# Decays as one exponential with masks as products, and reciprocal roots by GpSimd's power, in the second layer

## The chip, the cores and the metric

The kernel runs on one core of one Trainium2 chip. The metric is the device time of one execution in microseconds, as the median of several runs. The core has five engines that run their own instruction streams in order and wait for each other by semaphores: TensorE (PE, its weight loads shown as PEld), VectorE (DVE), ScalarE (ACT), GpSimd (POOL) and SyncE (SP, here only an issuer of DMAs).

## The reference

One inference step of two layers over 1088 frames: 1024 of a new stream and 64 of a running one, width 1024. The first layer (gated convolution and band attention) is not touched. The second is a gated delta rule with 8 heads of 128 in chunks of 64 frames:

```
q, k = l2norm(q) * 128**-0.5, l2norm(k)          # x * rsqrt(sum(x*x) + 1e-6)
gc = cumsum(g)                                    # g <= 0, within a chunk
decay[i, j] = exp(gc[i] - gc[j]) for j <= i, else 0
a = strictly lower part of beta[i] * (k k^T) * decay
u, w from solving (a + I) x = [v * beta, k * beta * exp(gc)]
u = u - w S
o = (q * exp(gc)) S + ((q k^T) * decay) u
S = exp(gc_last) * S + (k * exp(gc_last - gc))^T u
o = rmsnorm(o, onorm) ; y = (o * silu(z)) @ w_out  # rmsnorm: x * rsqrt(mean(x*x) + 1e-6) * onorm
```

What is computed must be seen: y of both streams, the caches of the first layer, the last convolution inputs and the state S of the second.

## The kernel before

Activations lie with features on the partitions and frames along the free axis, in three groups of 384, 384 and 320 frames. Every projection splits weights and inputs in a rounded and a remainder part and runs three matmuls per block of 128 x 128 (rows `pjt<-hhi,whi`, `pjt<-hlo,whi`, `pjt<-hhi,wlo`); these make up most of TensorE's work.

The mixer of the second layer takes its 8 heads as four pairs (p = 0 to 3, one head on each half of the partitions) and the 17 chunks of a pair in three batches of 6, 6 and 5 (`BATCHES`). Its steps are generators, and a class `Order` writes TensorE's instruction order out by hand: every step says after which others it may run, has a rank (a lower one goes first), and says with `yield ns` how long it leaves TensorE to others; the estimated time goes on with each matmul. The projections (`main`, rank 5) fill what the steps leave. TensorE keeps exactly this order; the orders of the other engines are made by the scheduler from its own estimate of times. All engines run their orders strictly, so an instruction that waits holds all behind it.

The steps, with the lines that the change and the prediction touch:

- `gates` (from line 885): cumulative decays gc and their exponentials for all pairs.
- `decays` (rank 3, after gates): for each pair and batch, VectorE multiplies gc with an identity (L926), a matmul with a block of ones spreads it over the rows into a bank "tr" of PSUM, VectorE subtracts gc into SBUF (`df`, L930), and for each of the two masks GpSimd adds or subtracts a mask of 0 and -1e30 (L933), ScalarE takes Exp (L934) and issues the write to DRAM (`Dd`, L935). The first is the decay for rows of a (j < i, called Dst), the second its transpose for q k^T (j >= i, called DT). The scratch tiles have one buffer each.
- `prepare` (rank 2, after the decays of its pair): loads Dst and DT through SP's queue, transposes k and q of the batch into "tr" banks, ScalarE sums their squares (`ss`, L976) and copies k (kt), VectorE scales k (kd). Then VectorE takes the reciprocal root of ss by a bit trick and three Newton steps (`rsqrt`, L774 to L780), forms the factors sT, sA and kap (L985 to L987), GpSimd scales kt (L988), TensorE forms k k^T and k q^T in a "tr" bank, and VectorE reads it into An (L997) and KQD (L998) with the decays. Af gathers the diagonal blocks of 16 (L1002, L1004) and goes to DRAM.
- `substitute`: reads the blocks back (AL) and inverts them on GpSimd in 28 small instructions (L1022, L1023), and writes them out again.
- `join`: reads them (Xf, X) and joins blocks of 16 to 64 with small matmuls.
- `solve`: forms u and w of all chunks.
- `scan` (rank 1): the recurrence over the chunks; each chunk's output o gets its sum of squares on ScalarE (`so`, L1144).
- `finish` (rank 3): for up to four chunks, forms the factor of rmsnorm together with q's norm: three VectorE instructions (L1200 to L1202), the bit trick on VectorE, three Newton steps on GpSimd (L782 to L785, twelve instructions), one more on VectorE (L1204); VectorE scales o (L1206), TensorE transposes it, ScalarE multiplies onorm in, and the result goes to DRAM.

The banks "tr" have two buffers, and all steps take them in turn: TensorE can write the next but one only when the engines have read out the present one.

Of the kernel before, what the change touches and what calls it, by code (L numbers as in the profile page):

```python
# [7 lines left out]
F32 = mybir.dt.float32  # L8
F32R = mybir.dt.float32r
I32 = mybir.dt.int32  # L10
AF = mybir.ActivationFunctionType
# [28 lines left out]
C_M1, C_M2 = 448, 512  # L40
# [16 lines left out]
def constants():  # L57
# [10 lines left out]
    c[:, C_M1:C_M1 + 64] = np.where(j[None, :] < i[:, None], 0.0, NEG)  # L68
    c[:, C_M2:C_M2 + 64] = np.where(j[None, :] >= i[:, None], 0.0, NEG)
# [38 lines left out]
class Net:  # L108
# [124 lines left out]
    def run(self):  # L233
# [4 lines left out]
        with tc.tile_pool(name="pj", bufs=2, space=PSUM) as self.pj:  # L238
# [15 lines left out]
            self.Dd = [dram.tile([P, NCH, 64], F32, name=f"Dd{i}") for i in range(8)]  # L254
# [505 lines left out]
    def odd(self):  # L760
# [12 lines left out]
        def rsqrt(out, x, tmp, eng):  # L773
            dve.tensor_scalar(out.bitcast(I32), x.bitcast(I32), 1, None, ALU.logical_shift_right)  # L774
            dve.tensor_scalar(out.bitcast(I32), out.bitcast(I32), -1, 0x5F3759DF, ALU.mult, ALU.add)  # L775
            for _ in range(3):
                if eng is dve:
                    dve.scalar_tensor_tensor(tmp, out, -0.5, x, ALU.mult, ALU.mult)
                    dve.tensor_tensor(tmp, tmp, out, ALU.mult)
                    dve.scalar_tensor_tensor(out, tmp, 1.5, out, ALU.add, ALU.mult)  # L780
                else:
                    pool.tensor_tensor(tmp, out, out, ALU.mult)  # L782
                    pool.tensor_tensor(tmp, tmp, x, ALU.mult)
                    pool.tensor_scalar(tmp, tmp, -0.5, 1.5, ALU.mult, ALU.add)
                    pool.tensor_tensor(out, out, tmp, ALU.mult)  # L785

# [125 lines left out]

        def decays():
            gc = G["gc"]
            buf = G["buf"]

            def part(i, m):
                return buf[:, 384 * i:384 * i + 64 * m].rearrange("p (c j) -> p c j", j=64)

            for p in range(4):  # L920
                yield 0
                for c0, m in BATCHES:
                    sh = [P, m, 64]
                    gcb = gc[:, p, c0:c0 + m].unsqueeze(2).broadcast_to(sh)
                    gx, df = part(0, m), part(1, m)
                    dve.tensor_tensor(gx, gcb, cst[:, C_ID64:C_ID64 + 64].unsqueeze(1).broadcast_to(sh), ALU.mult)  # L926
                    yield 900
                    ps = pst("tr")
                    self.mm(ps[:, :64 * m], cst[:, C_BD:C_BD + P], gx.rearrange("p c j -> p (c j)"))
                    dve.tensor_tensor(df, ps[:, :64 * m].rearrange("p (c j) -> p c j", j=64), gcb, ALU.subtract)  # L930
                    for q, (cm, op) in enumerate(((C_M1, ALU.subtract), (C_M2, ALU.add))):
                        dx = part(2 + q, m)
                        pool.tensor_tensor(dx, cst[:, cm:cm + 64].unsqueeze(1).broadcast_to(sh), df, op)  # L933
                        act.activation(dx, dx, AF.Exp)  # L934
                        nc.scalar.dma_start(Dd[2 * p + q][:, c0:c0 + m, :], dx)  # L935
                    yield 2500
                order.done.add(f"dec{p}")
# [4 lines left out]
        def zeroed():  # L942
            for name, w in (("Cb", 32), ("BD", P)):
                Z[name] = self.kp.tile([P, NBM, w], F32, name=name)
                pool.memset(Z[name], 0.0)

        def prepare(p, b):
# [3 lines left out]
            yield 4000 if b == 0 else 0  # L951
# [13 lines left out]
            rr = self.kp.tile([P, 2, NBM], F32, name="rr", tag="rr", bufs=3)[:, :, :nb]  # L965
# [398 lines left out]
```

## Time and profile before

| what | value |
|---|---|
| median of 3 runs | 1439.04 us (1437.8 to 1440.11) |
| profiled execution | 1441.69 us, its span 1439.9 us |
| TensorE busy | 1367.9 us, 95% of the span |
| VectorE, ScalarE, GpSimd busy | 867.4, 676.3, 304.9 us |
| mean clock granted to TensorE | 0.982 |
| mixer of the second layer | about 690 to 1310 us |
| decays within it (L926 to L935) | 691 to 774 us |

Times in a row are microseconds from the start of the span, and its length; a bracket at the end of a row tells how long the engine sat idle before it and whose end released it. "x" is the number of instructions. L12 is line 12 of the kernel; L119 and L124 are the helpers through which every matmul and transpose goes, so there the names of the tiles tell them apart.

### The profile page before, as it was taken

The numbers are of one execution on the slowest core, as the hardware profiler recorded it, in microseconds if no ns is written. First come the engines' busy times: TensorE is split into PE (matmuls) and PEld (weight loads), VectorE is DVE, ScalarE is ACT, GpSimd is POOL, SyncE is SP. The second block draws the span as 40 slices with busy tenths as digits, with TensorE's granted clock in tenths as the row PEclk, the third lists the DMA queues.
The fourth block names the chain that finished last, engine by engine and source line by source line (L and its number), as shares of the span: only waits on it lengthen the run. The fifth ranks groups of instructions, "written<-read, shape, count | busy, mean of one in ns | idle before, by whom it ended". The sixth has DMA issues, their size and how long they took to land. (4 is left out here: it accounts for less than half of the span.)

```text
span 1439.9 us, 28413 instructions
## 1 busy us (share of the span) xinstructions
PE 1367.9 (95%) x10600; PEld 1231.2 (86%) x10600; DVE 867.4 (60%) x2496; ACT 676.3 (47%) x1776; POOL 304.9 (21%) x805
## 2 busy tenths in 40 slices
PE   8999999999999999899889999999898989999996
PEld 6989998998999899788768777778786778889995
DVE  7675257237425754777787768666765765433554
ACT  7643345144334455676445554545443534333652
POOL 4001000000100014321235325140524151410222
PEclk9999999999999999999988999999999999999998
DMA  8403111210211274541433112121311142336753
GB/s 267 138 17 90 57 53 45 87 53 27 78 58 47 65 237 140 174 165 38 110 83 67 42 40 70 31 60 33 68 34 42 39 99 61 104 107 219 228 198 117
DMA packets 113834, 132.73 MB, mean 92 GB/s; under 512 B 35280, under 2 KB 80792, under 8 KB 113696
## 3 DMA queue, kind: packets, MB, share of 16 engines
q1 hardware_dynamic: 82448, 104.32, 24.8%
q10 hardware_dynamic: 31248, 26.60, 5.7%
q8 instruction: 83, 1.36, 0.4%
q14 instruction: 55, 0.45, 0.1%
HBM read 99.71 MB, written 34.31 MB: 93 GB/s over the span
## 5 line engine op out<-in xcount | busy, mean ns | idle before, releaser
L119 PE MATMUL pjt<-hhi,wlo 128*128 128x384 f32 (+1 forms) x1768 | 616.9, 349 | 2.8 <-DVE wlo L165 2.8
L119 PE MATMUL pjt<-hhi,whi 128*128 128x384 f32 (+1 forms) x1768 | 583.7, 330 | 10.0 <-ACT whi L164 4.8
L119 PE MATMUL pjt<-hlo,whi 128*128 128x384 f32 (+1 forms) x1768 | 575.9, 329 | 1.0 <-DVE hlo L418 0.9
L119 PEld LDWEIGHTS pjt<-hhi,wlo 128*128 128x128 f32 x1768 | 337.1, 191 | 27.0 <-issue 11.9
L119 PEld LDWEIGHTS pjt<-hhi,whi 128*128 128x128 f32 x1768 | 337.2, 191 | 16.6 <-ACT whi L164 5.8
L119 PEld LDWEIGHTS pjt<-hlo,whi 128*128 128x128 f32 x1768 | 335.5, 190 | 1.9 <-DVE hlo L418 1.9
L165 DVE TENSOR_TENSOR wlo<-wf,whi 128x512 fp32r<-128x512 f32 x222 | 152.5, 710 | 165.4 <-ACT whi L164 164.1
L164 ACT CAST whi<-wf 128x512 fp32r<-128x512 f32 x222 | 130.1, 619 | 166.9 <-PE pjt L119 122.4
L639 ACT ACTIVATE pr<-pr,mx 128x640 f32<-128x640 f32 (+5 forms) x72 | 50.9, 707 | 89.4 <-DVE mx L638 88.8
L811 DVE SCALAR_TENSOR_TENSOR kq<-pjt,par,kq 128x384 f32<-128x384 f32 (+2 forms) x144 | 71.6, 497 | 2.9
L600 POOL MEMSET bias<- 64x64 f32 x8 | 1.5, 182 | 320.7 <-DMA bias<-Gd 295.5
L375 POOL TENSOR_TENSOR sqa<-sqa,sq 128x384 f32<-128x384 f32 (+1 forms) x36 | 39.9, 1109 | 138.0 <-ACT sq L372 137.9
L636 DVE CUSTOM_DVE_ANT_0 pr<-sc,bias 128x640 f32<-128x640 f32 (+5 forms) x72 | 47.9, 666 | 26.8 <-PE sc L119 25.9
L1022 POOL TENSOR_TENSOR px<-AL 48x14 f32<-48x14 f32 (+6 forms) x168 | 46.1, 274 | 61.0 <-DMA AL<-Sd 52.0
L1185 DVE SCALAR_TENSOR_TENSOR S<-S,egl,su 128x128 f32<-128x128 f32 x128 | 40.6, 342 | 30.0 <-PE su L119 29.6
L782 POOL TENSOR_TENSOR so<-so 128x4 f32<-128x4 f32 (+2 forms) x72 | 17.1, 238 | 176.0 <-DVE so L775 117.6
L976 ACT ACTIVATE junk<-tr 128x128 f32<-128x128 f32 x136 | 37.7, 277 | 34.0 <-PE tr L124 28.9
L1023 POOL TENSOR_TENSOR AL<-AL,px 48x14 f32<-48x14 f32 (+6 forms) x168 | 46.2, 275 | 9.4
L124 PE MATMUL pt<-cst,pr 128*128 128x128 f32 (+1 forms) x280 | 43.3, 270 | 4.4 <-DVE pr L641 2.9
L1144 ACT ACTIVATE junk<-o 128x128 f32<-128x128 f32 x68 | 21.0, 309 | 50.8 <-DVE o L1140 40.9
L119 PE MATMUL pjt<-mhi,whi 128*128 128x384 f32 x128 | 43.0, 336 | 1.1 <-ACT whi L164 1.1
L119 PE MATMUL pjt<-mhi,wlo 128*128 128x384 f32 x128 | 43.0, 336 | 0.5 <-DVE wlo L165 0.5
(257 smaller groups left out, 2192.0 us busy)
## 6 DMA issues: line engine op xcount, KB each, us to landing
wf<-in_w_in SPq DMA_DIRECT2D x128, 256.0 KB, 3.7
wf<-in_w_out SPq DMA_DIRECT2D x96, 256.0 KB, 3.2
mf<-mixd SPq DMA_DIRECT2D x31, 192.0 KB, 4.5
x<-in_x SPq DMA_DIRECT2D x8, 384.0 KB, 5.8
xg<-in_x SPq DMA_DIRECT2D x2, 1536.0 KB
xd<-xg SPq DMA_DIRECT2D x2, 1536.0 KB
Dd<-dbuf ACTq DMA_DIRECT2D x16, 192.0 KB, 3.6
od<-o ACTq DMA_DIRECT2D x12, 256.0 KB, 2.3
```

The costliest lines, as they stand in the source:

```text
L119: return self.pe.matmul(out, lhsT=lhsT, rhs=rhs, start=start, stop=stop, **k)
L124: return self.pe.transpose(out, in_, self.ident[0:k, 0:k])
L164: self.act.copy(out=hi, in_=x)
L165: (eng or self.dve).tensor_tensor(lo, x, hi.bitcast(F32), ALU.subtract)
L375: pool.tensor_tensor(acc, acc, sq, ALU.add)
L636: dve.tensor_tensor_reduce(out=cut(pr[0:nq, :nk]), in0=sc[0:nq, :nk // nw, :nw], in1=cut(b["bias"][a][0:nq, j0:j0 + nk]), scale=1.0, scala ...
L639: act.activation(pr[0:nq, :nk], pr[0:nq, :nk], AF.Exp, bias=mx[0:nq, 1:2], scale=1.0, accum_out=mx[0:nq, 2:3])
L811: dve.scalar_tensor_tensor(oi, ch(ps[:, i0 + j + 1:i0 + j + 1 + m]), cw[j], oi, ALU.mult, ALU.add)
L976: act.activation(junk, ps[:, i, :], AF.Square, accum_out=ss[:, a, i0 + i:i0 + i + 1])
L1022: pool.tensor_tensor(t, AL[:, j + 1:16, j:j + 1].broadcast_to([lanes, m, w]), x.broadcast_to([lanes, m, w]), ALU.mult)
L1023: pool.tensor_tensor(o, o, t, ALU.add)
L1185: dve.scalar_tensor_tensor(Sn[:, q, :], S[:, q, :], egl[:, q, p, c:c + 1], su[q], ALU.mult, ALU.add)
```

## The change

The decay becomes one matrix per pair and batch, E = exp(-|gc_j - gc_i|), which serves both triangles, and the masks become products of 0 and 1:

- the subtraction writes back into its PSUM bank, ScalarE takes Abs from there to SBUF, and Exp with scale -1 in place;
- for pairs 1 to 3, `decays` writes E to DRAM once, with three scratch tiles in turn, and `prepare` loads it once; for pair 0, `prepare` computes E itself in its own tile, and waits for `gates` only;
- KQD starts as E times the upper mask, on GpSimd, and is multiplied with k q^T in place; An takes E unmasked, and Af is multiplied with the strictly lower mask of a 16 x 16 block on VectorE (later steps use only the blocks of An below the diagonal).

The reciprocal roots are taken by GpSimd with the operation `pow` and an exponent of -0.5 from a constant tile: one addition and one power in `prepare` for k, and the same in `finish`, where q's norm no longer needs a root of its own: rmsnorm's factor is (mean(o*o) + eq) ** -0.5 with eq = 128 * 1e-6 * (sum(q*q) + 1e-6). The mean's 1/128 moves into the scale of ScalarE's square.

```diff
-    c[:, C_M1:C_M1 + 64] = np.where(j[None, :] < i[:, None], 0.0, NEG)
-    c[:, C_M2:C_M2 + 64] = np.where(j[None, :] >= i[:, None], 0.0, NEG)
+    c[:, C_LOW:C_LOW + 16] = j[None, :16] < (i % 16)[:, None]
+    c[:, C_UP:C_UP + 64] = j[None, :] >= i[:, None]
...
+        def decay(e, gx, p, c0, m):
+
+            sh = [P, m, 64]
+            gcb = G["gc"][:, p, c0:c0 + m].unsqueeze(2).broadcast_to(sh)
+            dve.tensor_tensor(gx, gcb, cst[:, C_ID64:C_ID64 + 64].unsqueeze(1).broadcast_to(sh), ALU.mult)
+            yield 900
+            ps = pst("tr")[:, :64 * m]
+            self.mm(ps, cst[:, C_BD:C_BD + P], gx.rearrange("p c j -> p (c j)"))
+            ps = ps.rearrange("p (c j) -> p c j", j=64)
+            dve.tensor_tensor(ps, ps, gcb, ALU.subtract)
+            act.activation(e, ps, AF.Abs)
+            act.activation(e, e, AF.Exp, scale=-1.0)
+
         def decays():
...
-            for p in range(4):
-                yield 0
+            for p in range(1, 4):
                 for c0, m in BATCHES:
-                    gx, df = part(0, m), part(1, m)
-                    dve.tensor_tensor(gx, gcb, cst[:, C_ID64:C_ID64 + 64].unsqueeze(1).broadcast_to(sh), ALU.mult)
-                    yield 900
-                    ps = pst("tr")
-                    self.mm(ps[:, :64 * m], cst[:, C_BD:C_BD + P], gx.rearrange("p c j -> p (c j)"))
-                    dve.tensor_tensor(df, ps[:, :64 * m].rearrange("p (c j) -> p c j", j=64), gcb, ALU.subtract)
-                    for q, (cm, op) in enumerate(((C_M1, ALU.subtract), (C_M2, ALU.add))):
-                        dx = part(2 + q, m)
-                        pool.tensor_tensor(dx, cst[:, cm:cm + 64].unsqueeze(1).broadcast_to(sh), df, op)
-                        act.activation(dx, dx, AF.Exp)
-                        nc.scalar.dma_start(Dd[2 * p + q][:, c0:c0 + m, :], dx)
+                    e = piece(2 + i % 3, m)
+                    yield from decay(e, piece(i % 2, m), p, c0, m)
+                    nc.scalar.dma_start(Dd[p][:, c0:c0 + m, :], e)
+                    i += 1
                     yield 2500
...
+            Z["root"] = self.kp.tile([P, 1], F32, name="root")
+            pool.memset(Z["root"], -0.5)
...
         def prepare(p, b):
-            yield 4000 if b == 0 else 0
-            Dst, DT = bt("Dst", 64), bt("DT", 64)
-            nc.sync.dma_start(Dst, Dd[2 * p][:, c0:c0 + nb, :])
-            nc.sync.dma_start(DT, Dd[2 * p + 1][:, c0:c0 + nb, :])
+            E, An, KQD = bt("E", 64), bt("An", 64, 2), bt("KQD", 64, 3)
+            if p:
+                nc.sync.dma_start(E, Dd[p][:, c0:c0 + nb, :])
+            else:
+                yield from decay(E, An, p, c0, nb)
+            if b == 0:
+                yield 4000
...
-            dve.tensor_scalar(ss, ss, EPS, None, ALU.add)
-            rsqrt(rr, ss, tmp, dve)
+            dve.tensor_scalar(eq, ss[:, 1, :], EPS, 128.0 * EPS, ALU.add, ALU.mult)
+            pool.tensor_scalar(rk, ss[:, 0, :], EPS, None, ALU.add)
+            pool.tensor_tensor(rk, rk, Z["root"].broadcast_to([P, nb]), ALU.pow)
...
+            pool.tensor_tensor(KQD, E, cst[:, C_UP:C_UP + 64].unsqueeze(1).broadcast_to([P, nb, 64]), ALU.mult)
...
-                dve.tensor_tensor(KQD[:, i0:i0 + m, :], ps[:, :m, 64:128], DT[:, i0:i0 + m, :], ALU.mult)
+                dve.tensor_tensor(KQD[:, i0:i0 + m, :], ps[:, :m, 64:128], KQD[:, i0:i0 + m, :], ALU.mult)
...
+            dve.tensor_tensor(Af, Af, cst[:, C_LOW:C_LOW + 16].unsqueeze(1).broadcast_to([P, nb, 16]), ALU.mult)
...
-                act.activation(junk, o4[:, a, :], AF.Square, accum_out=so[:, 0, a:a + 1])
+                act.activation(junk, o4[:, a, :], AF.Square, scale=128.0 ** -0.5, accum_out=so[:, 0, a:a + 1])
...
         def finish(p, b, i0, m, o4, so):
-            rq = R[p, b]["rq"][:, i0:i0 + m]
-            va, fa, tm = so[:, 0, :m], so[:, 1, :m], so[:, 2, :m]
-            dve.scalar_tensor_tensor(va, va, 1.0 / (128.0 * 128.0), rq, ALU.mult, ALU.mult)
-            dve.tensor_tensor(va, va, rq, ALU.mult)
-            dve.tensor_scalar(va, va, EPS, None, ALU.add)
-            rsqrt(fa, va, tm, pool)
-            dve.scalar_tensor_tensor(fa, fa, 128.0 ** -0.5, rq, ALU.mult, ALU.mult)
+            fa = so[:, 1, :m]
+            pool.tensor_tensor(fa, so[:, 0, :m], R[p, b]["eq"][:, i0:i0 + m], ALU.add)
+            pool.tensor_tensor(fa, fa, Z["root"].broadcast_to([P, m]), ALU.pow)
...
-                order.add(f"prep{n}", 2, prepare(p, b), [f"dec{p}"] + after("prep", n - 1) + after("wy", n - 2) + after("scan", n - 3))
+                order.add(f"prep{n}", 2, prepare(p, b), [f"dec{p}" if p else "gates"] + after("prep", n - 1) + after("wy", n - 2) + after("scan", n - 3))
```

More of the change, by code (lines that the diff above doesn't have):

```diff
@@ L39 @@
 C_ID64 = 384
-C_M1, C_M2 = 448, 512
+C_LOW, C_UP = 448, 512
 C_B16 = 576
@@ L253, in run @@
             self.Gd = [dram.tile([P, LROW], F32, name=f"Gd{h}") for h in range(8)]
-            self.Dd = [dram.tile([P, NCH, 64], F32, name=f"Dd{i}") for i in range(8)]
+            self.Dd = [dram.tile([P, NCH, 64], F32, name=f"Dd{i}") for i in range(4)]
             self.Sd = [[dram.tile([m, P, 16], F32, name=f"Sd{a}{b}") for b, (c0, m) in enumerate(BATCHES)] for a in range(2)]
@@ L771, in comp @@
             return self.kp.tile([P, 4, NCH], F32, name=name)
[L773 to L785, printed above, removed]
         def ch(x):
@@ L981, in prepare @@
                     yield 2160
-            dve.tensor_scalar(ss, ss, EPS, None, ALU.add)
-            rsqrt(rr, ss, tmp, dve)
-            sT, sA, kap = small("sT"), small("sA"), small("kap")
-            dve.tensor_tensor(sT, beta[:, p, c0:c0 + nb], rr[:, 0, :], ALU.mult)
-            dve.scalar_tensor_tensor(sA, sT, -1.0, rr[:, 0, :], ALU.mult, ALU.mult)
-            dve.scalar_tensor_tensor(kap, egc[:, p, c0:c0 + nb], -1.0, rr[:, 0, :], ALU.mult, ALU.mult)
+            sT, sA, kap, rk, eq = (small(x) for x in ("sT", "sA", "kap", "rk", "eq"))
+            dve.tensor_scalar(eq, ss[:, 1, :], EPS, 128.0 * EPS, ALU.add, ALU.mult)
+            pool.tensor_scalar(rk, ss[:, 0, :], EPS, None, ALU.add)
+            pool.tensor_tensor(rk, rk, Z["root"].broadcast_to([P, nb]), ALU.pow)
+            dve.tensor_tensor(sT, beta[:, p, c0:c0 + nb], rk, ALU.mult)
+            dve.scalar_tensor_tensor(sA, sT, -1.0, rk, ALU.mult, ALU.mult)
+            dve.scalar_tensor_tensor(kap, egc[:, p, c0:c0 + nb], -1.0, rk, ALU.mult, ALU.mult)
             pool.tensor_tensor(kt, kt, kap.unsqueeze(2).broadcast_to([P, nb, P]), ALU.mult)
-            An, KQD = bt("An", 64, 2), bt("KQD", 64, 3)
+            pool.tensor_tensor(KQD, E, cst[:, C_UP:C_UP + 64].unsqueeze(1).broadcast_to([P, nb, 64]), ALU.mult)
             for i0 in range(0, nb, 4):
@@ L996, in prepare @@
                 for i in range(m):
-                    dve.scalar_tensor_tensor(An[:, i0 + i, :], ps[:, i, 0:64], sA[:, i0 + i:i0 + i + 1], Dst[:, i0 + i, :], ALU.mult, ALU.mult)
-                dve.tensor_tensor(KQD[:, i0:i0 + m, :], ps[:, :m, 64:128], DT[:, i0:i0 + m, :], ALU.mult)
+                    dve.scalar_tensor_tensor(An[:, i0 + i, :], ps[:, i, 0:64], sA[:, i0 + i:i0 + i + 1], E[:, i0 + i, :], ALU.mult, ALU.mult)
+                dve.tensor_tensor(KQD[:, i0:i0 + m, :], ps[:, :m, 64:128], KQD[:, i0:i0 + m, :], ALU.mult)
                 yield 510
@@ L1004, in prepare @@
                 dve.scalar_tensor_tensor(Af, An[:, :, 16 * j:16 * j + 16], cst[:, C_B16 + j:C_B16 + j + 1], Af, ALU.mult, ALU.add)
+            dve.tensor_tensor(Af, Af, cst[:, C_LOW:C_LOW + 16].unsqueeze(1).broadcast_to([P, nb, 16]), ALU.mult)
             sa = Sd[0][b]
             nc.sync.dma_start(sa.rearrange("c r j -> r c j"), Af)
-            R[p, b] = dict(kd=kd, kt=kt, KQD=KQD, rq=rr[:, 1, :], An=An, sT=sT)
+            R[p, b] = dict(kd=kd, kt=kt, KQD=KQD, eq=eq, An=An, sT=sT)
             yield 0
@@ L1154, in scan @@
                     o4 = self.kp.tile([P, 4, P], F32, name="o4", tag="o4", bufs=3)
-                    so = self.kp.tile([P, 3, 4], F32, name="so", tag="so", bufs=3)
+                    so = self.kp.tile([P, 2, 4], F32, name="so", tag="so", bufs=3)
                 c = c0 + i
```

9 lines of the change are left out of this document (2 added, 7 removed).

## The prediction

> **What bounds the kernel now.** I read the page first, then the windows of the two parts of the second layer's mixer, then who waited for whom on TensorE, then the timelines around its longest gaps.
>
> ```profile
> span 1439.9 us, 28413 instructions
> PE 1367.9 (95%) x10600; PEld 1231.2 (86%) x10600; DVE 867.4 (60%) x2496; ACT 676.3 (47%) x1776; POOL 304.9 (21%) x805
> 690.00:772.00 82.00, 65.90 (x358) 57.98 (x357) 65.64 (x165) 40.73 (x118) 35.50 (x55) 0.88 0.34 94
> 772.00:1310.00 538.00, 516.14 (x5148) 434.02 (x5147) 340.32 (x1243) 235.70 (x790) 166.55 (x642) 0.98 0.25 61
> ```
>
> TensorE bounds: its order is written out, and the steps that the diff touches run between 690 and 1310 us. The change keeps TensorE's number of matmuls (twelve of the decays, as before), so it can only act through TensorE's idle time and its clock. The columns after the length are TensorE, weight loads, VectorE, ScalarE, GpSimd, then the clock. While the decays run (690 to 772) TensorE is idle for 82.0 - 65.9 = 16.1 us and its clock is 0.88; in the rest of the mixer it is idle for 21.9 us of 538. These 38 us and the slow clock are all there is to win.
>
> Who ends the waits, first while the decays run, then behind them (us in total, times, longest):
>
> ```profile
> PE tr L124 <- DVE KQD L998: 3.4, 1, 3.4
> PE tr L124 <- DVE dbuf L930: 3.4, 2, 2.6
> PE tr L119 <- DVE KQD L998: 3.3, 1, 3.3
> PE tr L119 <- ACT junk L976: 2.8, 2, 2.2
> PE tr L119 <- DVE dbuf L926: 1.5, 2, 1.1
> ...
> PE tr L124 <- DVE o L1206: 4.5, 2, 3.0
> PE su L119 <- DVE us L1171: 4.0, 2, 2.7
> PE tr L124 <- DVE KQD L998: 2.4, 3, 1.2
> PE tr L124 <- ACT M L1081: 2.2, 2, 1.4
> PE tr L119 <- DVE KQD L998: 1.3, 5, 0.3
> ```
>
> Most name a "tr" bank of PSUM (two buffers) that a later step of prepare, decays or finish has not yet read out. TensorE's timeline shows what a long one costs beside itself:
>
> ```profile
> 733.20 0.30 PE L119 MATMUL pjt<-hhi,whi 128*128 128x320 f32 x1
> 733.35 0.31 PE L119 MATMUL pjt<-hlo,whi 128*128 128x320 f32 x1
> 737.09 1.09 PE L124 MATMUL tr<-cst,kq 128*128 128x128 f32 x4 [3.44 <-DVE KQD L998]
> 738.25 0.47 PE L119 MATMUL pjt<-hhi,whi 128*128 128x320 f32 x1
> 738.51 0.47 PE L119 MATMUL pjt<-hlo,whi 128*128 128x320 f32 x1
> ...
> 742.46 0.79 PE L124 MATMUL tr<-cst,kq 128*128 128x128 f32 x4
> ...
> 762.15 1.62 PE L119 MATMUL tr<-dbuf,cst 128*128 128x384 f32 x2 [3.29 <-DVE KQD L998]
> 766.45 0.45 PE L119 MATMUL pjt<-hhi,whi 128*128 128x320 f32 x1
> 766.71 0.33 PE L119 MATMUL pjt<-hlo,whi 128*128 128x320 f32 x1
> ```
>
> Matmuls that started 0.15 us apart start 0.26 us apart behind the 3.44 us gap, until about 742.7; behind the 3.29 us gap the same until about 766.6. Each slow stretch loses 44% of its length: 5.6 x 0.44 = 2.5 and 4.45 x 0.44 = 2.0 us.
>
> **Part 1: the roots of prepare.** The path from the sums of squares to the release of the bank, on VectorE, and GpSimd beside it:
>
> ```profile
> 728.51 0.17 DVE L774 TENSOR_SCALAR rr<-ss 128x12 int32<-128x12 int32 x1
> 730.91 0.98 DVE L779 TENSOR_TENSOR rt<-rt,rr 128x12 f32<-128x12 f32 x1
> 733.51 0.17 DVE L985 TENSOR_TENSOR sT<-beta,rr 128x6 f32<-128x6 f32 x1
> 735.77 0.85 DVE L997 SCALAR_TENSOR_TENSOR An<-tr,sA,Dst 128x64 f32<-128x64 f32 x4
> 730.66 2.17 POOL L933 TENSOR_TENSOR dbuf<-cst,dbuf 128x384 f32<-128x384 f32 x2 [2.21 <-DVE dbuf L930]
> ```
>
> Eleven instructions of the root (2 + 3 x 3) take 733.51 - 728.51 = 5.0 us, because other work of VectorE stands between them and because some take 0.98 instead of 0.17 us while GpSimd's mask runs. They become an addition and a power on GpSimd. No row shows a power. The nearest are GpSimd's small products (first row below), the longest GpSimd instruction of the mixer is the third:
>
> ```profile
> L782 POOL TENSOR_TENSOR so<-so 128x4 f32<-128x4 f32 x36 | 8.3, 232 | 149.2 <-DVE so L775 91.9 <-DVE rt L779 36.5 <-DVE rr L780 19.2
> L933 POOL TENSOR_TENSOR dbuf<-cst,dbuf 128x384 f32<-128x384 f32 x16 | 18.2, 1151 | 60.1 <-DVE dbuf L930 53.0 <-DMA Dd<-dbuf 6.9
> L988 POOL TENSOR_TENSOR kt<-kt,kap 128x768 f32<-128x768 f32 x8 | 11.7, 1467 | 35.6 <-DVE sA L986 34.6 <-DVE kap L987 1.0
> POOL px L1022 <- DMA AL<-Sd: 52.0, 12, 9.8
> ```
>
> So a power lies between 0.23 and 1.47 us; I take 0.23, the same form and nearly the same width. With two handovers the new path is some 0.7 us, and up to 1.9: 3 to 4.3 us shorter than 5.0. Both long KQD waits (3.4 and 3.3) fit into that: -6.7 us, and -4.5 us of slow clock. Of the later ones 2.4 go as -2.0, and the five of 0.3 stay. GpSimd runs in order, so the root can stand behind substitute's first product, which waits for its DMA (52.0 us over 12 waits, last row); that is the danger of this part.
>
> The Trainium skill, "TensorE: Matmul & The Clock Gate", Part 1, says that the array goes to half speed after an idle window of about 3.4 us. By that rule only the 3.44 us gap would have slowed it, the slow clock would be worth 2.5 instead of 4.5 us here and nothing in part 3, and the forecast would be about 1432; the rows show it after 3.29 us as well, so I go by the rows.
>
> **Part 2: the decays.** Gone are 24 GpSimd masks of 1.15 us, twelve of the 24 Exps, and most of the writes to DRAM and reads back (24 of each become nine). In their place stand twelve Abs, twelve GpSimd products for KQD (1.15 us each, off the path, since E is there long before the sums of squares) and one VectorE product on Af ahead of substitute's DMA (some 0.2 to 0.3 us by L997's 0.85 for four tiles of 64; hidden while TensorE projects, 12 x 0.3 = 3.6 us if that cover is gone). For the first pair the whole decay (two VectorE, a matmul, two ScalarE) moves into prepare, with no DMA; that batch's prepare then waits only for the gates and starts about three pieces earlier, past nothing on SP but its own two loads. An earlier start doesn't move an end that TensorE's total work sets: nothing. What can move is the bank:
>
> ```profile
> 753.63 0.47 ACT L934 ACTIVATE dbuf<-dbuf 128x320 f32<-128x320 f32 x1 [3.21 <-POOL dbuf L933]
> L930 DVE TENSOR_TENSOR dbuf<-tr,gc 128x384 f32<-128x384 f32 x8 | 4.4, 554 | 4.1 <-PE tr L119 2.4 <-POOL dbuf L933 1.7
> L372 ACT ACTIVATE sq<-pjt x42: 414/483/512, 528.2 to 1428.7; 128x384 f32<-128x384 f32 x28, 128x320 f32<-128x320 f32 x14
> ```
>
> Here ScalarE stood 3.21 us for a mask that was behind substitute on GpSimd, the squares queued behind it, and TensorE waited 2.2 us for them (the "junk" row): with the masks gone, -2.2. Against that, the subtraction now leaves its result in the bank, which comes free only after Abs: 0.48 us as the square from PSUM (the last row), with the handover 0.55, and up to 3.2 more where ScalarE stands as above. Twice in twelve pieces TensorE waited for this bank already (L930, 3.4 us). I charge 0.55 us to six of the twelve: +3.3; the ends are 0, and 12 x 1.5 = +18 if ScalarE is late each time.
>
> **Part 3: finish.** Six VectorE and twelve GpSimd instructions for each of 24 groups become two GpSimd ones.
>
> ```profile
> 1165.33 0.19 POOL L782 TENSOR_TENSOR so<-so 128x4 f32<-128x4 f32 x1
> 1170.27 0.20 POOL L785 TENSOR_TENSOR so<-so 128x4 f32<-128x4 f32 x1
> 1172.11 0.87 DVE L1206 TENSOR_SCALAR o<-o,so 128x128 f32<-128x128 f32 x4
> 1160.00:1180.00 20.00, 15.53 (x143) 13.39 (x143) 13.61 (x60) 5.63 (x19) 11.87 (x48) 0.91 0.46 112
> ```
>
> The twelve took 1165.33 to 1170.47 = 5.1 us, interleaved with substitute and kt; two take half a microsecond, so L1206 comes over 4 us earlier than TensorE's waits for it (3.0 and 1.5): -4.5, and 0.09 x 15.5 = -1.4 of clock.
>
> **The sum.** -6.7 - 4.5 - 2.0 - 2.2 + 3.3 - 4.5 - 1.4 = -18.0 us. What is late next: TensorE reaches the following bank that much sooner, and VectorE, busy 65.6 of 82 us in this part, uses TensorE's gaps to catch up; behind 772 the waits on L1171 and L1081 (4.0 and 2.2) aren't touched and fall anew. I let half of the gain go there: -9 us. The profiled execution took 1441.7 us (1.8 around its span), the median run 1439.0; -9 on the median is 1430.
>
> **The rivals.** *All of it stays*: the gaps go and none opens, as the lighter VectorE and GpSimd speak for: -18, 1421. *The gaps only move*: TensorE is 95% busy and every gap refills; for it speaks that 26 short gaps of many causes make up the 21.9 us behind 772: 1439. *The bank is held through ScalarE*: Abs stands in ScalarE's order behind a copy that itself waits for TensorE, and TensorE waits for the bank. At 1.5 us on each of twelve pieces this is +18 in place of +3.3, less half of the other terms' 21.3 (-10.7): +7, 1446. It decides from a hold of 0.9 us per piece, where twelve of them eat the 10.7; against it speaks the 2.5 us pause that the order leaves behind each piece. *The power is slow*: nothing bounds it but rows of other functions. At 5 us it takes back the whole of part 1's path; at 10 us each of twelve prepares is 5 us later, and if a third of that reaches TensorE the time is 1439 + 20 = 1459. The Trainium skill, "GPSIMD Engine Reference", 4.1 Engine selection, advises VectorE and not GpSimd for elementwise work, at about half its speed; at 0.23 against 0.17 us these small tiles show little of that. *The change doesn't do what it says* has no room: every edit replaces instructions that the trace has.
>
> **How the numbers follow.** Forecast (-4 to -15) 0.50; all stays 0.15; gaps move (within 3) 0.16; bank held 0.11; slow power 0.08. About 0.2%, 2.9 us, is what a measurement of this kernel can tell from no change. Faster 0.65, same 0.16, slower 0.19. The range leaves out the slow power, the far end of the held bank and of the case that all stays: 1417 to 1447.
>
> **What would show it.** Right: no KQD wait over 1 us on TensorE before 772, none for L1206's successor over 0.5; the clock between 690 and 772 above 0.92; powers under 1.5 us; the first transposes of prepare some 10 us earlier. Part 2's charge shows as TensorE's waits for Abs. Wrong: long waits of VectorE for the power, a power behind a DMA wait on GpSimd, or idle time of TensorE in the mixer of 38 us or more.

## The result, and the profile after

The changed kernel takes 1449.67 us (median of 4, 1444.78 to 1452.40) against 1438.42 us of the kernel before beside it. The ratio is 1.0061, 95% interval [1.0037, 1.0086]; the quotient of the two medians, 1.0078, lies inside it. It is slower by 0.6% where 0.6% faster was forecast. A later series with the unchanged text gave 1.0033 [1.0003, 1.0062]. The profiled execution took 1444.78 us and is the fastest of the four, so the trace shows the slowdown only in part.

The first two lines of its page (span, then busy time by engine):

```profile
span 1443.0 us, 27858 instructions
...
PE 1371.1 (95%) x10600; PEld 1235.2 (86%) x10600; DVE 833.1 (58%) x2232; ACT 675.4 (47%) x1774; POOL 274.7 (19%) x578
```

VectorE and GpSimd are lighter by 34 and 30 us, as the change says, and TensorE's idle time is what it was: 1439.9 - 1367.9 = 72.0 us before, 1443.0 - 1371.1 = 71.9 now. The 3.1 us of this execution are busy time, which for the same 10600 matmuls means a slower clock: its mean over the span is 0.978, and 0.982 before. The trace of the later series says the same (71.0 us idle, clock 0.976). The windows of the mixer (columns as before):

```profile
690.00:772.00 82.00, 69.97 (x553) 62.83 (x552) 61.86 (x173) 43.28 (x128) 26.26 (x70) 0.96 0.22 59
772.00:1310.00 538.00, 510.27 (x4935) 427.94 (x4935) 311.58 (x975) 233.84 (x779) 146.65 (x398) 0.97 0.22 55
```

While the decays run, TensorE gains 4.1 us and the clock goes from 0.88 to 0.96. Behind 772 us it loses more: idle for 27.7 us in place of 21.9, at 0.97 in place of 0.98. Over both windows the idle time rises from 38.0 to only 39.8 us, so these two traces alone don't show where the 11 us between the medians are lost; the experiments below are needed for that. What they show is that other waits stand in the place of the old ones. Who ends the waits of TensorE, in the first window and then in the second:

```profile
PE tr L119 <- ACT vt L1112: 4.4, 1, 4.4
PE tr L119 <- DVE KQD L990: 4.2, 2, 3.7
PE tr L119 <- DVE dbuf L903: 1.7, 1, 1.7
PE tr L124 <- ACT dbuf L909: 1.2, 1, 1.2
PE tr L124 <- DVE kd L970: 0.4, 1, 0.4
```

```profile
PE tr L119 <- DVE XT L1045: 9.1, 3, 4.6
PE tr L119 <- DVE KQD L990: 7.4, 8, 5.3
PE tr L124 <- DVE o L1133: 2.6, 2, 1.4
PE tr L124 <- DVE o L1195: 2.1, 1, 2.1
PE su L119 <- DVE us L1164: 0.9, 1, 0.9
PE tr L119 <- ACT E L909: 0.8, 1, 0.8
```

A long KQD wait stands before 772 us (3.7 us), a longer one has come at 1166 us (5.3), and there is a cause that hardly stood among the waits before: XT, the input of `join`, 9.1 us. In this kernel L909 is Abs, L976 and L1193 are the two powers, L1195 scales o (L1206 before), L980 scales kt, L1044 and L1045 make X and XT, L1015 and L1016 are substitute's products.

The powers, by form (GpSimd's groups of the mixer; the KQD mask, L981, and the addition ahead of the power, L1192, for comparison):

```profile
L1193 POOL TENSOR_TENSOR so<-so,root 128x4 f32<-128x4 f32 x12 | 12.2, 1015 | 0.8
L976 POOL TENSOR_TENSOR rk<-rk,root 128x6 f32<-128x6 f32 x8 | 10.8, 1349 | 0.4
L981 POOL TENSOR_TENSOR KQD<-E,cst 128x384 f32<-128x384 f32 x8 | 8.1, 1008 | 101.6 <-ACT E L910 59.0 <-PE tr L119 24.2 <-DMA E<-Dd 10.6
L1193 POOL TENSOR_TENSOR so<-so,root 128x2 f32<-128x2 f32 x8 | 5.6, 696 | 0.6
L976 POOL TENSOR_TENSOR rk<-rk,root 128x5 f32<-128x5 f32 x4 | 5.1, 1266 | 0.3
...
L1192 POOL TENSOR_TENSOR so<-so,eq 128x4 f32<-128x4 f32 x12 | 2.4, 199 | 75.8 <-ACT junk L1137 75.8
L1193 POOL TENSOR_TENSOR so<-so,root 128x1 f32<-128x1 f32 x4 | 2.2, 548 | 0.1
```

From 0.55 us for one column to 1.35 us for six: about 0.4 us and 0.16 us for each column; 12.2 + 10.8 + 5.6 + 5.1 + 2.2 = 35.9 us for the 36 of them. An addition of the same shape takes 0.20 us. A power of six columns costs more than the mask over 384. What stands around one pair of them, from the timeline of all engines:

```profile
1158.73 0.24 POOL L975 TENSOR_SCALAR rk<-ss 128x6 f32<-128x6 f32 x1
...
1159.30 1.34 POOL L976 TENSOR_TENSOR rk<-rk,root 128x6 f32<-128x6 f32 x1
...
1160.67 0.25 DVE L977 TENSOR_TENSOR sT<-beta,rk 128x6 f32<-128x6 f32 x1 [2.94 <-POOL rk L976]
...
1161.27 1.01 POOL L1193 TENSOR_TENSOR so<-so,root 128x4 f32<-128x4 f32 x1
...
1162.31 2.42 DVE L1195 TENSOR_SCALAR o<-o,so 128x128 f32<-128x128 f32 x4 [0.83 <-POOL so L1193]
1162.51 1.46 POOL L980 TENSOR_TENSOR kt<-kt,kap 128x768 f32<-128x768 f32 x1
...
1164.65 0.85 DVE L989 SCALAR_TENSOR_TENSOR An<-tr,sA,E 128x64 f32<-128x64 f32 x4
...
1165.98 1.12 PE L119 MATMUL tr<-kq 128*64 128x128 f32 x8 [5.29 <-DVE KQD L990]
```

VectorE stands 2.94 us for the first power and 0.83 us for the second; the scaling of o, which the scheduler put ahead of An, takes 2.42 us beside kt's product; so An starts at 1164.65 and TensorE waits 5.29 us for the bank. How much of such a gap is the power's length can't be read from these rows; the run with a short product in its place (below) shows that it is little. The other new wait, XT at 898 us, runs over SP's queue:

```profile
891.29 0.32 SPq L1020 DMA_DIRECT2D Sd<-AL  x1
...
894.44 0.38 SPq L1032 DMA_DIRECT2D Xf<-Sd  x1
...
896.56 0.65 POOL L1044 TENSOR_TENSOR X<-Xf,cst 128x96 f32<-128x96 f32 x2 [5.30 <-DMA Xf<-Sd]
...
897.77 0.83 PE L119 MATMUL tr<-XT,Cb 32*32 32x16 f32 x48 [4.61 <-DVE XT L1045]
```

Here the write of substitute's result is issued at 891.29, its reading back 3.15 us later, and TensorE joins it at 897.77, when TensorE has stood for 4.61 us. Substitute itself is longer in the first batch of the second, third and last pair (15.2, 14.1 and 16.7 us from the first product's start to the last one's end, 9.4, 10.3 and 11.1 before), but not of the first pair (13.6, and 15.5 before). The first and the last of its products for the last pair, in the trace of after and in that of before:

```profile
1155.11 0.21 POOL L1015 TENSOR_TENSOR px<-AL 48x14 f32<-48x14 f32 x1 [6.48 <-DMA AL<-Sd]
...
1171.63 0.21 POOL L1016 TENSOR_TENSOR AL<-AL,px 48x14 f32<-48x14 f32 x1
```

```profile
1157.79 0.21 POOL L1022 TENSOR_TENSOR px<-AL 48x14 f32<-48x14 f32 x1 [9.80 <-DMA AL<-Sd]
...
1168.69 0.21 POOL L1023 TENSOR_TENSOR AL<-AL,px 48x14 f32<-48x14 f32 x1
```

It takes 1171.84 - 1155.11 = 16.7 us in place of 11.1. Three powers (1.34 + 1.01 + 0.55 us) and the KQD mask (0.87) stand between its instructions, and GpSimd stands idle among them for 1.60 us ahead of an addition of finish, which waits for ScalarE, and for 0.66 us ahead of the mask, which waits for E's load. The product on kt stands there in both kernels, and six small ones of finish's Newton steps did before.

### The profile page after: what moved, and what is told of

It reads as the page before. It is cut to its first block, busy times and chain, and to the rows that moved or that the text cites. A ratio compares the mean times of both kernels' runs of the same rounds, so it can differ in the third digit from the quotient of the medians.

```text
span 1443.0 us, 27858 instructions
## 1 busy us (share of the span) xinstructions
PE 1371.1 (95%) x10600; PEld 1235.2 (86%) x10600; DVE 833.1 (58%) x2232; ACT 675.4 (47%) x1774; POOL 274.7 (19%) x578
## 5 line engine op out<-in xcount | busy, mean ns | idle before, releaser
L119 PEld LDWEIGHTS pjt<-hhi,whi 128*128 128x128 f32 x1768 | 338.4, 191 | 12.2 <-ACT whi L164 5.2
L1015 POOL TENSOR_TENSOR px<-AL 48x14 f32<-48x14 f32 (+6 forms) x168 | 45.5, 271 | 27.7 <-DMA AL<-Sd 16.2
L1016 POOL TENSOR_TENSOR AL<-AL,px 48x14 f32<-48x14 f32 (+6 forms) x168 | 47.6, 283 | 11.8
L119 PE MATMUL ks<-S,kq 128*64 128x128 f32 x512 | 43.1, 290 | 0.0
```

The costliest lines, as they stand in the source:

```text
L119: return self.pe.matmul(out, lhsT=lhsT, rhs=rhs, start=start, stop=stop, **k)
L1015: pool.tensor_tensor(t, AL[:, j + 1:16, j:j + 1].broadcast_to([lanes, m, w]), x.broadcast_to([lanes, m, w]), ALU.mult)
L1016: pool.tensor_tensor(o, o, t, ALU.add)
```

## The experiments

Ratios are to the kernel before on the same chip, with their 95% intervals; each is known to about 0.25%, a quotient of two of them to about 0.4%. In the experiments' series the kernel before took 1446.4 to 1449.4 us (medians) and not 1438, so an expected time is read here as a ratio: 1438 us is 1.000, and 1446 to 1452 us is 1.005 to 1.009. Two theories came first: that the power's length, on GpSimd and in the path of prepare, takes the gain (A), and that the new way of the decays does, through the held bank or through TensorE's changed order (B). TensorE's instruction order is told with each kernel, since `Order` writes it from estimated times and a step that starts elsewhere moves many others. The scheduler then makes the other engines' orders anew as well, so a new order of TensorE is always a new order of all of them, and no run here varies TensorE's alone.

### The parts, each with the rest unchanged

Decays of the changed kernel, roots as before (order of TensorE as in the changed kernel):

```diff
-            pool.tensor_scalar(rk, ss[:, 0, :], EPS, None, ALU.add)
-            pool.tensor_tensor(rk, rk, Z["root"].broadcast_to([P, nb]), ALU.pow)
+            dve.tensor_scalar(ss, ss, EPS, None, ALU.add)
+            rsqrt(rr, ss, tmp, dve)
...
+            rsqrt(fa, va, tm, pool)
```

> The decays of the changed kernel with the roots of before (Newton steps); TensorE's order is that of the changed kernel. Theory A: 1438 or less, since no power is left. Theory B: 1446 to 1452.

Measured: 1463.87 us, 1.0119 [1.0094, 1.0145]: against theory A, and slower still than theory B had it. The decays alone, with the first pair's in prepare, make the kernel slower, and most of it comes through a wait that nothing of the decays is part of: TensorE's waits for the scaled o (L1214 here) are 22.5 us in place of 4.5, the longest this one:

```profile
898.19 1.09 PE L124 MATMUL tr<-cst,o 128*128 128x128 f32 x4 [10.05 <-DVE o L1214]
```

In this order finish's transposes come where Newton's twelve steps aren't done. Here the powers help: with them the kernel is at 1.003 to 1.006.

Roots of the changed kernel, decays as before (order as before):

```diff
-            dve.tensor_scalar(ss, ss, EPS, None, ALU.add)
-            rsqrt(rr, ss, tmp, dve)
+            pool.tensor_scalar(rk, ss[:, 0, :], EPS, None, ALU.add)
+            pool.tensor_tensor(rk, rk, Z["root"].broadcast_to([P, nb]), ALU.pow)
...
-            rsqrt(fa, va, tm, pool)
+            pool.tensor_tensor(fa, fa, Z["root"].broadcast_to([P, m]), ALU.pow)
```

> The roots of the changed kernel with the decays of before; TensorE's order is that of before. Theory A: 1445 to 1455. Theory B: below 1436, since the two long KQD waits and the ones on finish go as forecast and nothing comes in their place.

Measured: 1451.02 us, 1.0020 [1.0000, 1.0040]: no gain, and between the bands of both theories. The KQD waits before 772 are gone, as forecast (3.0 us of them are left in the mixer, the longest 0.6, in place of 10.4), though the power has its full length here. In their place stands a wait for XT:

```profile
776.76 0.84 PE L119 MATMUL tr<-XT,Cb 32*32 32x16 f32 x48 [9.51 <-DVE XT L1038]
```

The changed kernel with both powers replaced by a product of the same shape with 0.001 (no root is taken; order as in the changed kernel):

```diff
-            pool.tensor_tensor(rk, rk, Z["root"].broadcast_to([P, nb]), ALU.pow)
+            pool.tensor_tensor(rk, rk, Z["root"].broadcast_to([P, nb]), ALU.mult)
```

> The changed kernel with both powers replaced by a product with 0.001, so that no root is taken; TensorE's order is that of the changed kernel to the instruction. It takes away 12 x 1.1 and 24 x 0.6 us of GpSimd's time and nothing else. Theory A (the power's length on GpSimd is the price: VectorE waits for it, and substitute's stream behind it gets longer): 1438 or less, 11 us under the changed kernel's 1450. Theory B (the decays are the price: the bank held through ScalarE, TensorE's new order): within 4 us of 1450.

Measured: 1434.60 us, 0.9919 [0.9893, 0.9945]. With the duration that the forecast had assumed for the power, the change is faster than before by 0.8%, near the forecast's 0.6%, as theory A says. So in this order the length of the 36 powers (its GpSimd is busy 247.7 us, 27 less than with them) is worth 1.1 to 1.4%. But the number agrees and the way doesn't: TensorE's waits for KQD are 10.8 us here, 10.4 before and 11.6 with the powers. The three gaps looked at above are still there:

```profile
741.58 0.66 PE L119 MATMUL tr<-kq 128*64 128x128 f32 x8 [3.00 <-DVE KQD L990]
900.98 0.84 PE L119 MATMUL tr<-XT,Cb 32*32 32x16 f32 x48 [4.57 <-DVE XT L1045]
1159.63 1.12 PE L119 MATMUL tr<-kq 128*64 128x128 f32 x8 [4.65 <-DVE KQD L990]
```

They come with the order; the power's length adds 0.7, 0.0 and 0.6 us to them. Ahead of the last one VectorE stands 3.39 us for the short product, longer than the 2.94 us for the power. What the short product takes away is most of the two shorter waits for XT (5.1 us of such waits in all, in place of 9.1; substitute's 16.7 us are 11.3) and of the one for the scaled o (0.7 in place of 2.1). TensorE's idle time over the whole span is 66.9 us in place of 71.9, at a mean clock of 0.983 in place of 0.978.

The changed kernel with prepare's root by Newton's steps on VectorE, the power in finish alone (order as in the changed kernel):

```diff
-            pool.tensor_scalar(rk, ss[:, 0, :], EPS, None, ALU.add)
-            pool.tensor_tensor(rk, rk, Z["root"].broadcast_to([P, nb]), ALU.pow)
+            dve.tensor_scalar(ss[:, 0, :], ss[:, 0, :], EPS, None, ALU.add)
+            rsqrt(rk, ss[:, 0, :], small("rt"), dve)
```

> The changed kernel with the root of prepare (k alone) by Newton steps on VectorE; finish keeps its power on GpSimd; TensorE's order is that of the changed kernel. If the power inside prepare's path is what costs (with no power at all 0.9919): 0.995 to 0.999. If it is the power's length on GpSimd as a whole, or finish alone: 1.003 or more.

Measured: 1438.53 us, 0.9948 [0.9922, 0.9973], 0.85 to 1.1% faster than the changed kernel: most of the power's price is that of prepare's.

### The first pair through DRAM, in the order of before

The changed kernel with the first pair's decays in the decays step, like the others:

```diff
-            for p in range(1, 4):
+            for p in range(4):
+                yield 0
...
+            yield 4000 if b == 0 else 0
...
-            if p:
-                nc.sync.dma_start(E, Dd[p][:, c0:c0 + nb, :])
-            else:
-                yield from decay(E, An, p, c0, nb)
-            if b == 0:
-                yield 4000
+            nc.sync.dma_start(E, Dd[p][:, c0:c0 + nb, :])
...
-                order.add(f"prep{n}", 2, prepare(p, b), [f"dec{p}" if p else "gates"] + after("prep", n - 1) + after("wy", n - 2) + after("scan", n - 3))
+                order.add(f"prep{n}", 2, prepare(p, b), [f"dec{p}"] + after("prep", n - 1) + after("wy", n - 2) + after("scan", n - 3))
```

> The changed kernel with pair 0's decays made in the decays step and sent through DRAM like the others; TensorE's order is that of before to the instruction. Theory B in its second form (the earlier start and TensorE's new order are the price, not the work): below 1440. Theory A, and theory B in its first form (the bank held through ScalarE): 1446 to 1452.

Measured: 1442.74 us, 0.9966 [0.9950, 0.9982], theory B in its second form. TensorE's order is that of before again, instruction by instruction, and the kernel is 0.7 to 0.95% faster than the changed one. The same with Newton's roots in both places (only the decays are changed against before):

```diff
-            pool.tensor_tensor(rk, rk, Z["root"].broadcast_to([P, nb]), ALU.pow)
...
+            rsqrt(rr, ss, tmp, dve)
...
-            pool.tensor_tensor(fa, fa, Z["root"].broadcast_to([P, m]), ALU.pow)
...
+            rsqrt(fa, va, tm, pool)
```

> One exponential and masks as products, nothing else: roots by Newton steps and pair 0's decays through DRAM, so TensorE's order is that of before to the instruction. If the lighter decays are a gain by themselves (as the step from roots alone, 1.0020, to roots with these decays, 0.9966, says): 0.993 to 0.997 of before. If they are a gain only beside the power: 1.000 or more.

Measured: 1432.00 us, 0.9908 [0.9885, 0.9932]: one exponential and the masks as products are worth 0.9% alone, more than expected. The same with the power in finish and Newton's steps in prepare, as against the kernel with both powers:

```diff
-            pool.tensor_scalar(rk, ss[:, 0, :], EPS, None, ALU.add)
-            pool.tensor_tensor(rk, rk, Z["root"].broadcast_to([P, nb]), ALU.pow)
+            dve.tensor_scalar(ss[:, 0, :], ss[:, 0, :], EPS, None, ALU.add)
+            rsqrt(rk, ss[:, 0, :], small("rt"), dve)
```

> The changed kernel with the first pair's decays in the decays step, through DRAM, and with prepare's root of k by Newton's steps on VectorE; only finish takes its root by the power. TensorE's written order is that of before. It stands beside two kernels with the same order: both roots by power (0.9966 of before) and both by Newton's steps (0.9908). If the power's length in prepare is what a late start of the first pair leaves over as a price, this kernel is at 0.988 to 0.992; if any power that stands in GpSimd's order is a price there, also that of finish, it is at 0.993 to 0.997; if what the start of the first pair costs and what the power costs are one and the same, it can't be told from 0.9966.

Measured: 1429.80 us, 0.9859 [0.9832, 0.9887]: the first case, a little below its band. In the order of before the parts are then: decays -0.9%, the power in finish -0.5% (0.9859 / 0.9908, just outside the uncertainty), the power in prepare +1.1% (0.9966 / 0.9859). Together they are 0.9966, still faster than before; the changed kernel has them all and lies above 1. What is left over, 0.7 to 0.95%, comes with the first pair's decays in prepare and the order that goes with them.

The waits for XT of the last kernel and of the one with both powers:

```profile
PE tr L119 <- DVE XT L1057: 8.6, 2, 6.2
```

```profile
PE tr L119 <- DVE XT L1042: 18.3, 3, 7.6
```

Before had 0.8 us of it, the kernel with Newton's roots in both places none. So part of what the powers save elsewhere comes back at `join`: with the power in prepare the waits for XT are 9.7 us more, while those for KQD are fewer (4.8 us in place of 9.0), and substitute's first batch of the last pair takes 15.3 us in place of 13.4. Not all of it is GpSimd's work: how soon substitute's result can be read back after its write varies too (last section).

### The order of TensorE

If only the early start of the first pair cost, a pause ahead of its decays should win it back. The changed kernel with a pause of 10.2 us of the order's time:

```diff
+                if b == 0:
+                    yield 10200
                 yield from decay(E, An, p, c0, nb)
```

> The changed kernel, unaltered, beside the three others on one chip. The single run so far gave 1.0061 of the kernel before; here 1.004 to 1.009.

> The changed kernel with one pause of 10.2 us of TensorE's estimated time ahead of pair 0's first batch, as long as three pieces took in the decays step; pair 0's decays still are made in prepare. If the earlier start is the price of the changed kernel: 0.995 to 0.999 of before, like the kernel with pair 0 through DRAM (0.9966). If making them in prepare is the price (the bank and VectorE in prepare's own path): 1.004 or more.

Measured: the changed kernel again 1450.49 us, 1.0033 [1.0003, 1.0062]; with the pause 1432.03 us, 0.9902 [0.9877, 0.9926]. Two lines of pace, the same work, and 1.3% (0.9902 / 1.0033): faster than either case had it. The windows with the pause show 4.5 us idle before 772 in place of 12.0, and only one wait for XT is left in the mixer, of 0.7 us:

```profile
690.00:772.00 82.00, 77.52 (x593) 70.75 (x593) 67.12 (x183) 44.73 (x130) 24.62 (x65) 0.96 0.31 65
772.00:1310.00 538.00, 514.74 (x4984) 431.22 (x4983) 313.03 (x975) 238.03 (x787) 150.75 (x404) 0.98 0.25 59
```

The decays are still made in prepare, with Abs from the bank: the held bank of theory B isn't what took the gain. It looked like the early start; the next three ask whether it is. The pause of 10.2 us with Newton's steps in prepare (edit as above; the order is the same as with the power), and pauses of 20.4 and 5.1 us:

```diff
-                    yield 10200
+                    yield 20400
```

```diff
-                    yield 10200
+                    yield 5100
```

> The kernel with the pause of 10.2 us ahead of the first pair's decays (0.9902 of before), with prepare's root of k by Newton's steps in place of the power; TensorE's order is the same instruction by instruction. If the early start and the power in prepare are two prices that add up, it is 0.5 to 0.9% faster than with the power: 0.981 to 0.985. If both act through the same late bank, which the pause has already given time, it can't be told from 0.9902 (0.988 to 0.993).

> The kernel with the pause, at 20.4 us in place of 10.2. If what the pause gives is that the first pair's prepare no longer stands among the work it was started into, a longer pause gives the same or somewhat less: 0.988 to 0.996 of before. If the pause of 10.2 us helped only because it happened to place matmuls well, another length has no reason to help: 0.999 to 1.007, as the changed kernel itself.

> The kernel with the pause at 5.1 us in place of 10.2. If the early start is the cause, half the pause gives a part of the gain: 0.992 to 1.000 of before. If the placing is chance, it can lie anywhere between 0.988 and 1.008, and with the pause of 20.4 us it shows no order by length.

Measured: 1435.39 us, 0.9902 [0.9871, 0.9934]; 1447.71 us, 0.9993 [0.9972, 1.0013]; 1457.84 us, 1.0064 [1.0039, 1.0090]. With no pause, 5, 10 and 20 us the time is 1.003 to 1.006, 1.006, 0.990 and 0.999: no order by length, and at 10.2 us the power in prepare costs nothing (with Newton's steps there the ratio is the same). Each order meets another late result. The longest gap with 5.1 us, then that with 20.4 us:

```profile
783.38 0.69 PE L119 MATMUL tr<-vt,KQD 64*64 64x128 f32 x4 [7.42 <-ACT E L909]
```

```profile
889.69 0.69 PE L119 MATMUL tr<-us,KQD 64*64 64x128 f32 x4 [10.06 <-DVE kd L972]
```

If so, a shift must move the kernel before as well. The first pair's prepare 5.1 and 10.2 us later in the kernel before, and in the best kernel so far:

```diff
-            yield 4000 if b == 0 else 0
+            yield (4000 if p else 9100) if b == 0 else 0
```

```diff
-            yield 4000 if b == 0 else 0
+            yield (4000 if p else 14200) if b == 0 else 0
```

> The kernel before with the first pair's prepare started 5.1 us later in TensorE's written order, nothing else changed. If the earlier start of the changed kernel is a cause by itself, a later start of an unchanged kernel moves it little: 0.997 to 1.003 of before. If every shift draws anew which late result TensorE meets, it lies anywhere between 0.985 and 1.015, as likely outside 0.996 to 1.004 as in it.

> As the run before, at 10.2 us later: 0.997 to 1.003 if the earlier start is the cause, anywhere between 0.985 and 1.015 and not in line with the run at 5.1 us if every shift draws anew.

> The kernel with one exponential, the first pair's decays through DRAM, Newton's steps in prepare and the power in finish (0.9859 of before), its first prepare 5.1 us later. If the earlier start is the cause, it stays at 0.983 to 0.990; if every shift draws anew, it lies between 0.98 and 1.003, and since 0.986 was the best of all so far, more likely above 0.990 than below 0.983.

> As the run before, at 10.2 us later: 0.983 to 0.990, or between 0.98 and 1.003.

Measured: the kernel before 1471.10 us, 1.0159 [1.0130, 1.0189], and 1468.14 us, 1.0136 [1.0103, 1.0168]; the best kernel 1443.68 us, 0.9970 [0.9946, 0.9994], and 1427.04 us, 0.9852 [0.9825, 0.9879]. A shift of 5.1 us in an order, with no other change, costs the kernel before 1.6%, just beyond the wider of the two expected bands. Its two longest gaps then:

```profile
744.14 1.40 PE L119 MATMUL tr<-dbuf,cst 128*128 128x320 f32 x2 [6.05 <-DVE KQD L998]
...
1199.31 1.09 PE L124 MATMUL tr<-cst,o 128*128 128x128 f32 x4 [8.94 <-DVE o L1206]
```

Both name the results that the forecast's two largest terms were about, KQD and the scaled o, at other places and longer. So the early start is no cause by itself: every shift draws anew which late result TensorE meets. Idle time and slow clock together are what tells all these kernels apart: in the 18 traces the span, less TensorE's idle time, less the share of the span that the granted clock falls short of 1, is between 1335 and 1345 us (before 1439.9 - 72.0 - 0.018 x 1439.9 = 1342), while the spans go from 1428 to 1472. The ratios by order of TensorE (the kernels of one row have the same instruction order on TensorE; the roots alone, 1.0020, belong to the first row, and the short product, 0.9919, to the fourth):

```
first pair's prepare    before's code   changed decays and   changed decays and   changed decays
                                        both Newton          power in finish      and both powers
as before               1               0.9908               0.9859               0.9966
5.1 us later            1.0159          -                    0.9970               -
10.2 us later           1.0136          -                    0.9852               -
as in the change        -               1.0119               0.9948               1.0033, 1.0061
 and pause 5.1 us       -               -                    -                    1.0064
 and pause 10.2 us      -               -                    0.9902               0.9902
 and pause 20.4 us      -               -                    -                    0.9993
```

In each of the three rows where both were run, the lighter decays with the power in finish beat the kernel before, by 1.4, 1.9 and 2.8% (0.9970 / 1.0159, 0.9852 / 1.0136). The gain of the parts is real, and the kernel before stands at the best of its three placements. The change as a whole leaves that placement and puts a slow power into prepare; the two together cost more than its gain. Either alone would have left it faster than before: 0.9966 with the powers in the old order, 0.9919 with the short product in the new one.

## Why the prediction was wrong

It said 1430 us (1417 to 1447), and 1449.67 lies beyond the range. By its own steps:

- *"An earlier start doesn't move an end that TensorE's total work sets: nothing."* This failed, and it is the step that counts most. The first transposes of prepare came earlier, by 5.1 us (here the row before, then after) and not by some 10, and with them TensorE's whole order through the mixer changed:

```profile
710.87 0.60 PE L124 MATMUL tr<-cst,kq 128*128 128x128 f32 x4
```

```profile
705.77 0.60 PE L124 MATMUL tr<-cst,kq 128*128 128x128 f32 x4
```

  The step took the gaps of the old order as the ones that the new kernel would have. TensorE's work did stay, but which results it waits for is drawn anew: 0.7 to 0.95% for this order against that of before (10 to 14 us of 1447), and 0.990 to 1.006 for the same work at four paces. With the pause of 10.2 us the decays stand in prepare as well and the loss is gone, so it is the order and not the new place of the work.
- *"I take 0.23, the same form and nearly the same width"* failed in size. The power took 1.35 us for six columns, within the bounds (0.23 to 1.47) but at the other end, and 1.02 for four. The form of the row says nothing of the function. Its path by the rows above, 1158.73 to 1160.67, is 1.9 us, the upper bound given.
- *"Both long KQD waits (3.4 and 3.3) fit into that: -6.7 us"* held for the order that it was read from and failed for the new one. In the order of before both are gone, even with the slow power (the longest KQD wait left is 0.6 us). In the changed order 4.2 us stand before 772 with the power and 3.0 with a product as short as was assumed, and over the mixer 11.6 and 10.8 us, no less than the 10.4 before. So it isn't the power's length that kept them.
- The slow power was priced as a rival from 5 us on, through VectorE's wait. At 1.35 us it already costs 1.1% in the order of before. The traces put more of that on a late XT than on VectorE's wait. VectorE waits 7.8 us in all for the powers of prepare, and 4.8 for the short products. TensorE's waits for KQD are 0.8 us more with the powers than with the short products in the changed order, and 4.2 us fewer with the power in prepare than without it in the old one; the waits for XT are 4.0 and 9.7 us more. No run tries the two ways apart. *"The root can stand behind substitute's first product; that is the danger of this part"* named the neighbour but not the direction: by the rows substitute stands behind the root as well, and XT is late (9.1 us of waits, 5.1 with the short products; in the order of before 8.6 without and 18.3 with the power in prepare).
- *Part 2's bank*: +3.3 us charged, and TensorE's waits for Abs are 1.2 + 0.8 = 2.0 us. Right. The squares' wait (*-2.2*) is gone, right. But the decays as a whole are worth -0.9%, 13 us in the order of before, where the terms gave a loss of 1.1 us. Which of the lighter GpSimd, the halved Exps and the fewer DMAs gives it wasn't tried apart.
- *Part 3, -4.5*: the power in finish is worth -0.5% or 7 us in the order of before, right in sign and roughly in size; the wait for L1195 that stays is 2.1 us against 4.5 before, where none over 0.5 was to be left.
- *The clock*, over 0.92 in the first window: it is 0.96. The direction is right: 0.08 of 70 busy us are 5.6 us, against 4.5 forecast. Behind 772 it fell by 0.01, which over 538 us takes back about 5 (two rounded figures). But the slow clock at 762 us was read wrongly as the price of the 3.29 us gap: in the trace of before the granted clock is 0.50 from 756.50 to 758.86 already, ahead of that gap and behind one of 2.21 us, and also from 719.0 to 722.3, behind one of 2.57 us.
- *"I let half of the gain go there"*: the direction was right, the size not. The trace shows the gains before 772 us (idle from 16.1 to 12.0) and the losses behind (from 21.9 to 27.7). Of the rivals, *the gaps only move* (1439 us, 0.16) comes nearest in mechanism; but it didn't allow for moved gaps that are dearer than the old ones. One of the signs given for a wrong forecast is there: TensorE's idle time in the mixer is 39.8 us, over the 38 named.

What stays open: why one order meets a gap of 7 us and another doesn't. Each gap could be read (a bank, XT, the scaled o), but no run tells which pace is good without trying it, and the price of the power in prepare (+1.1% in one order, 0.9 to 1.1% in the second, none in the third) depends on it.

The version that came of it, one exponential and masks as products with all pairs through DRAM, Newton's steps in prepare and the power in finish, takes 0.9859 of before, and with 10.2 us of pause 0.9852, which can't be told from it.

## What to carry to other kernels

Where an order is written out from estimates, a change that moves a step is a change of the whole order: run the new code in the old order, and old and new at two or three other paces, before its parts are judged; here the pace alone is worth up to 1.6%, as much as the change. An operation that no row shows is priced by the far bound until it is measured, and its price falls on what stands behind it on its engine, not only on who waits for its result. And combine parts by what each is worth alone: of this change two helped (0.9 and 0.5%), one took back 1.1%, and the new order took the rest.

## What the runs showed of the hardware

- A power on GpSimd is about three to six times as dear as an addition of the same shape (0.55 against 0.19 us for one column, 1.02 against 0.20 for four, 1.35 against 0.24 for six) and grows by 0.16 us with each column (0.55, 0.70, 1.02, 1.35 us for 1, 2, 4 and 6 columns of 128 partitions); a product over 384 columns took 1.01 us.
- The scaling of o on VectorE, of 68 instructions (shortest, median and longest in ns):

```profile
L1195 DVE TENSOR_SCALAR o<-o,so x68: 274/279/1740, 797.5 to 1299.2; 128x128 f32<-128x128 f32 x68
```

  The longest, 1740 ns, is the median and 1461 more, which is the whole length of kt's product on GpSimd that started beside it at 1162.51 (1.46 us): VectorE didn't share, it stood. The Trainium skill, "SBUF — State Buffer", Who interferes with whom, says that a VectorE instruction in a two-port mode, which a `tensor_scalar` can enter, contends with GpSimd, and that the one that issues first has the shared ports for its whole instruction while the other blocks fully. The trace agrees on the full block; by its recorded starts VectorE's instruction was the earlier one, at 1162.31, so it doesn't bear out which of the two must wait.
- The load that reads substitute's result back waits on SP for the write of 48 or 40 KB. With the pause of 10.2 us, the longest and the shortest of the twelve:

```profile
1099.49 0.30 SPq L1022 DMA_DIRECT2D Sd<-AL  x1
1104.57 0.38 SPq L1034 DMA_DIRECT2D Xf<-Sd  x1
...
1224.71 0.30 SPq L1022 DMA_DIRECT2D Sd<-AL  x1
1226.17 0.37 SPq L1034 DMA_DIRECT2D Xf<-Sd  x1
```

  From 1.46 to 5.08 us for the same 40 KB. What the long ones collide with wasn't looked into.
- The granted clock falls to half behind gaps of TensorE of 2.2 to 3.0 us already: 0.50 behind 2.21 and 2.57 us in the kernel before (above), and 0.50 from 1039.3 to 1045.5 us behind 2.96 us in the changed one. Behind one of 2.10 us at 882.45 in the changed kernel it stays at 1.00; what else decides wasn't looked into.
